# Strassen's scheme, one level, for the two feed-forward products of a transformer-like layer on one Trainium2 core

## The chip, the core and the metric

The kernel runs on one core of a Trainium2 chip. The core has five engines that run side by side, each through its own list of instructions from the first to the last: TensorE (PE) for matrix products and transposes, VectorE (DVE), ScalarE (ACT), GpSimd (POOL) and SyncE (SP). SP does no arithmetic here; it issues transfers between the chip's memory (DRAM) and SBUF, the core's working memory. TensorE writes to PSUM, eight banks of 128 x 512 float32. Engines wait for each other through semaphores. The metric is the device time of one execution in microseconds; lower is better.

## The reference, cut to what matters

One layer on 1024 tokens with 1024 channels: a normed projection, three mixers (a gated convolution, a stick-breaking attention, a cross-attention into 256 memory tokens), their gated sum, an output projection, and then the feed-forward part:

```python
        x = x + merged @ w_out[l]

        h2 = rms_norm(x, g_mlp[l])
        x = x + jnp.square(jax.nn.relu(h2 @ w_up[l])) @ w_down[l]
```

Here `h2` is 1024 x 1024, `w_up` 1024 x 4096 and `w_down` 4096 x 1024. The change touches only these two products and what surrounds them.

## The kernel before, in words

**Operands.** Every float32 operand is kept as two fp32r parts, a rounded part (hi) and what rounding left (lo). One product of a 128 x 128 block by a 128 x 512 block is three matmuls: hi by hi, hi by lo, lo by hi (`mm3` and `mm3_steps`, lines 125 to 127 and 205 to 207). To make the two parts, ACT copies with rounding (line 89 for a loaded weight of 128 x 1024, line 113 elsewhere) and DVE subtracts (lines 90 and 114). A product of weights therefore waits for ACT, and then for DVE behind ACT.

**Pools.** Weights are loaded by SP into `raw` (4 buffers of 128 x 1024), their two parts go to `whl` (3 buffers, each holding both parts of one load). Nearly everything else lives in `pg`, 40 pages of 128 x 1024 float32. PSUM is dealt out as `d` (3 banks), `z` (2), `t` (2) and `o` (1). Short-lived 128 x 512 tiles are in `hp` (3 buffers).

**Order.** The kernel's text is a recording: a scheduler turns it into one list for each engine, in the order of the text as far as buffers and its own estimate of times allow. The lists are fixed before the program runs, and an engine that waits at one row does none of the rows behind it.

**The output projection** (line 794) adds `merged @ w_out` to the rows of `x`, eight tiles of 128 rows (`acc`, one page each, kept in SBUF to the end). As each of them is done in its second half, `normed` (lines 157, 146, 150, 159) makes the normed row tile. `norm_transpose` (line 178 on PE, lines 116 and 117 for the two parts) turns the row tiles into `h2`, first those of the first 512 tokens, woven into the last tiles of the output projection, then those of the other 512, woven into the first matmuls of the feed-forward part.

**The feed-forward part** is a loop over 8 chunks of 512 inner columns. For each chunk: four blocks of 128 inner columns, each by two token halves, eight k-blocks and three matmuls (192 matmuls); ACT takes relu (line 812) and the square's hi part (line 815), DVE squares (816) and subtracts (817). Then, for two column halves and eight token tiles, four inner blocks by three matmuls (192 matmuls), and DVE adds the bank to `acc` (line 833). The inner result never leaves SBUF. In the last chunk each half tile of `acc` goes out as soon as its add is done (line 835). In all there are 3072 matmuls of 128x512.

Of the kernel before, what the change touches and what calls it, by code (L numbers as in the profile page):

```python
# [16 lines left out]
P = 128  # L17
# [5 lines left out]
NXH = 4  # L23
NM = M // P
FF = 4096
NCHUNK = FF // 512
EPS = 1e-6


# [7 lines left out]
def f32v(ap):  # L37

    return ap.bitcast(F32)
# [3 lines left out]
def block_kernel(ctx, tc, x, mem, small, w_in, w_v, w_kv, w_co, w_so, w_xo, w_out, w_up, w_dn, out):  # L43
# [19 lines left out]
    def page(dt=F32R, shape=(P, 1024)):  # L63
        return pgp.tile(list(shape), dt, tag="pg", name=nm("pg"))
# [41 lines left out]
    def unit(src, paged=False):  # L106

        return halves(load(src), paged)
# [63 lines left out]
    def norm_transpose(rows, dst, gcol):  # L172

        n = len(rows) * P
        for k in range(KT):
            tp = pt()
            for i, r in enumerate(rows):
                nc.tensor.transpose(tp[:, i * P : (i + 1) * P], r[:, k * P : (k + 1) * P], ident)
# [576 lines left out]

    acc = [None] * 8
    rows = []
    h2 = [None] * KT

    def h2_dst(th):  # L760
        def dst(k):
            if th == 0:
                h2[k] = {}
            t_ = page(F32R, (P, 2, 512))
            h2[k][th] = (t_[:, 0, :], t_[:, 1, :])
            return h2[k][th]

        return dst

    for ch in range(2):  # L770
        s = slice(ch * 512, ch * 512 + 512)
        while len(wo) < 4 * ch + 4:
            wo.append(unit(w_out[ch, len(wo) - 4 * ch], True))
        for t in range(8):
            th, i = t // 4, t % 4
            if ch == 0:
                acc[t] = page(F32)
                nc.sync.dma_start(out=acc[t], in_=x[t * P : (t + 1) * P, :])
            ps = pd()
            steps = mm3_steps(  # L780
                ps,
                [
                    (cut(mT[k, th], i * P, (i + 1) * P), cut(wo[4 * ch + k // 2], (k % 2) * 512, (k % 2) * 512 + 512))
                    for k in range(KT)
                ],
                4,
            )
            if ch == 1 and t == 5:
                more = norm_transpose(rows[0:4], h2_dst(0), C_GMLP)
# [10 lines left out]
    for c in range(NCHUNK):  # L800
        f = {}
        for j2 in range(2):
            ws = [unit(w_up[4 * c + 2 * j2 + j]) for j in range(2)]
            for th, j in ((0, 0), (0, 1), (1, 0), (1, 1)):
                w = ws[j]
                ps = pd()
                steps = mm3_steps(ps, [(cut(w, k * P, (k + 1) * P), h2[k][th]) for k in range(KT)], KT)
                if (c, j2, th, j) == (0, 0, 0, 1):
                    weave(steps, norm_transpose(rows[4:8], h2_dst(1), C_GMLP))
                run(steps)  # L810
                r = hpp.tile([P, 512], F32, tag="hp", name=nm("r"))
                nc.scalar.activation(r, ps, AF.Relu)
                t_ = page(F32R, (P, 2, 512))
                f[2 * j2 + j, th] = (t_[:, 0, :], t_[:, 1, :])
                nc.scalar.activation(t_[:, 0, :], r, AF.Square)
                nc.vector.tensor_tensor(out=r, in0=r, in1=r, op=ALU.mult)
                nc.vector.tensor_tensor(out=t_[:, 1, :], in0=r, in1=f32v(t_[:, 0, :]), op=ALU.subtract)
        for ch in range(2):
            us = [unit(w_dn[c, ch, kp]) for kp in range(2)]
            s = slice(ch * 512, ch * 512 + 512)  # L820
            for t in range(8):
                ps = pd()
                mm3(
                    ps,
                    [
                        (
                            cut(f[j, t // 4], (t % 4) * P, (t % 4 + 1) * P),
                            cut(us[j // 2], (j % 2) * 512, (j % 2) * 512 + 512),
                        )
                        for j in range(4)  # L830
                    ],
                )
                nc.vector.tensor_tensor(out=acc[t][:, s], in0=ps, in1=acc[t][:, s], op=ALU.add)  # L833
                if c == NCHUNK - 1:
                    nc.sync.dma_start(out=out[t * P : (t + 1) * P, s], in_=acc[t][:, s])


def _layout(i):
# [10 lines left out]
    def per_part(v):  # L849
# [9 lines left out]
    w_dn = a["w_down"][0].reshape(NCHUNK, 2, 2, P, 2, 512).transpose(0, 4, 1, 3, 2, 5)  # L859
    return {  # L860
        "x": a["x"][0],
        "mem": a["mem"][0],
# [9 lines left out]
        "w_dn": w_dn.reshape(NCHUNK, 2, 2, P, 1024),  # L872
    }


# [17 lines left out]
```

## Time and profile before

| what | value |
| --- | --- |
| time, median of 3 runs | 2309.98 us (2309.84 to 2311.8) |
| the profiled execution's own time | 2309.64 us |
| its span in the profile | 2307.9 us |
| PE busy | 2261.2 us (98% of the span) |
| DVE, ACT, POOL busy | 1130.1, 803.3, 303.3 us |
| bytes moved | 174.79 MB, mean 76 GB/s |
| last matmul of the output projection starts | 1603.44 us |
| last matmul of all starts | 2303.57 us |

In the profile a row of a group of instructions gives the line, the engine, the operation, what it writes and reads, the shape, the count, and then busy time in us, the mean of one in ns, and the engine's idle time just before such instructions with what ended it. The time of a matmul in these rows is from its start to its end; successive matmuls overlap, so their spacing has to be read from counts in a window. A row of the timeline gives the start and the duration in us.

### The profile page before, as it was taken

What the parts mean: (1) busy time and instruction counts of PE and PEld (TensorE: products, weight loads), DVE (VectorE), ACT (ScalarE), POOL (GpSimd) and SP (SyncE); (2) the same over time, 40 slices, a digit from 0 to 9 for tenths busy, and PEclk for the clock granted to TensorE, in tenths of its full rate; (3) what the DMA queues carried; (4) which work ended last, traced back from release to release, by engine and by line L of the source; (5) the groups of instructions that cost most, each with busy time, mean ns of one, the idle gap of its engine ahead of it and who ended that gap; (6) DMA issues with size and microseconds to landing.
All of it is one profiled execution on the core that took longest, in us unless ns stands there. A gap on an engine that the chain in (4) does not pass through costs nothing.

```text
span 2307.9 us, 26972 instructions
## 1 busy us (share of the span) xinstructions
PE 2261.2 (98%) x10688; PEld 1880.7 (81%) x10688; DVE 1130.1 (49%) x1589; ACT 803.3 (35%) x1550; POOL 303.3 (13%) x422
## 2 busy tenths in 40 slices
PE   7999999999999999999999999999999999999999
PEld 6988888778778778788888888888888888888887
DVE  5534127787777777763333344443333333333333
ACT  6544235565556555541122121223221221221221
POOL 1021113333334333320000000000000000000000
PEclk9999999999999999999999999999999999999999
DMA  6311322222122122211111443250111111111111
GB/s 220 101 60 68 125 69 76 72 75 81 64 83 73 65 90 65 83 40 52 46 47 63 146 156 128 92 191 1 37 55 55 37 55 52 40 55 48 44 46 73
DMA packets 49455, 174.79 MB, mean 76 GB/s; under 512 B 6065, under 2 KB 6065, under 8 KB 49329
## 3 DMA queue, kind: packets, MB, share of 16 engines
q1 hardware_dynamic: 42160, 147.90, 20.4%
q0 software_dynamic: 7168, 25.17, 2.9%
q8 instruction: 84, 1.38, 0.2%
q14 instruction: 43, 0.34, 0.0%
HBM read 135.29 MB, written 29.36 MB: 71 GB/s over the span
## 4 chain that ended last, share of the span: by engine, by line
PE 82%; DVE 6%; issue 5%; POOL 4%; ACT 3%; DMA 1%; SPq 0%; POOLq 0%; ACTq 0%; DVEq 0%
PE d L205 16%; PE d L207 16%; PE d L206 16%; PE d L125 9%; PE d L127 9%; PE d L126 9%; POOL pg L558 3%; PE o L597 2%; DVE pg L114 1%; PE t L582 1%; DVE pg L572 1%; ACT pg L555 1%; PE z L554 1%; PE z L553 1%; DVE pg L568 1%
## 5 line engine op out<-in xcount | busy, mean ns | idle before, releaser
L205 PE MATMUL d<-pg,whl 128*128 128x512 f32 x1664 | 655.2, 394 | 0.0
L207 PE MATMUL d<-pg,whl 128*128 128x512 f32 x1664 | 649.8, 391 | 0.0
L206 PE MATMUL d<-pg,whl 128*128 128x512 f32 x1664 | 649.4, 390 | 0.0
L207 PEld LDWEIGHTS d<-pg,whl 128*128 128x128 f32 x1664 | 312.4, 188 | 66.5
L206 PEld LDWEIGHTS d<-pg,whl 128*128 128x128 f32 x1664 | 312.7, 188 | 60.1
L205 PEld LDWEIGHTS d<-pg,whl 128*128 128x128 f32 x1664 | 312.7, 188 | 60.1
L90 DVE TENSOR_TENSOR whl<-raw,whl 128x1024 fp32r<-128x1024 f32 x160 | 201.9, 1262 | 302.3 <-ACT whl L89 301.8
L89 ACT CAST whl<-raw 128x1024 fp32r<-128x1024 f32 x160 | 168.6, 1054 | 518.4 <-PE d L127 291.5
L558 POOL TENSOR_SCALAR_AFFINE_SELECT pg<-pg 128x128 f32<-128x128 f32 x256 | 181.2, 713 | 317.4 <-ACT pg L555 301.6
L568 DVE TENSOR_TENSOR_SCAN pg<-pg,zero 128x128 f32<-128x128 f32 (+7 forms) x128 | 176.2, 1377 | 64.3 <-POOL pg L558 62.6
L127 PE MATMUL d<-whl,pg 128*128 128x512 f32 x512 | 199.2, 389 | 0.0
L125 PE MATMUL d<-whl,pg 128*128 128x512 f32 x512 | 199.2, 389 | 0.0
L126 PE MATMUL d<-whl,pg 128*128 128x512 f32 x512 | 199.2, 389 | 0.0
L113 ACT CAST pg<-t 128x256 fp32r<-128x256 f32 (+2 forms) x336 | 115.2, 364 | 212.4 <-DVE pg L114 144.7
L833 DVE TENSOR_TENSOR pg<-d,pg 128x512 f32<-128x512 f32 x128 | 88.3, 690 | 188.8 <-PE d L127 188.5
L114 DVE TENSOR_TENSOR pg<-t,pg 128x256 fp32r<-128x256 f32 (+2 forms) x336 | 129.4, 404 | 69.6 <-ACT pg L113 66.2
L126 PE MATMUL d<-pg,whl 128*128 128x512 f32 x384 | 149.4, 389 | 0.0
L125 PE MATMUL d<-pg,whl 128*128 128x512 f32 x384 | 149.4, 389 | 0.0
L127 PE MATMUL d<-pg,whl 128*128 128x512 f32 x384 | 149.4, 389 | 0.0
L205 PE MATMUL d<-pg,pg 128*128 128x512 f32 (+1 forms) x384 | 138.1, 360 | 1.3 <-ACT pg L116 1.3
L206 PE MATMUL d<-pg,pg 128*128 128x512 f32 (+1 forms) x384 | 136.9, 357 | 0.5 <-DVE pg L90 0.5
L207 PE MATMUL d<-pg,pg 128*128 128x512 f32 (+1 forms) x384 | 136.9, 357 | 0.0
(114 smaller groups left out, 2747.3 us busy)
## 6 DMA issues: line engine op xcount, KB each, us to landing
raw<-in_w_in SPq DMA_DIRECT2D x72, 512.0 KB, 3.6
raw<-in_w_up SPq DMA_DIRECT2D x32, 512.0 KB, 3.7
raw<-in_w_dn SPq DMA_DIRECT2D x32, 512.0 KB, 4.3
gscr<-pg POOLq DMA_DIRECT2D x24, 512.0 KB, 2.9
raw<-gscr SPq DMA_DIRECT2D x24, 512.0 KB, 3.3
raw<-in_w_kv SPq DMA_DIRECT2D x16, 512.0 KB, 4.4
pg<-in_x SPq DMA_DIRECT2D x16, 512.0 KB, 8.2
pg<-pg SPq DMA_DIRECT2D x32, 256.0 KB, 3.4
```

Of the source, the lines that this page charges most:

```text
L89: a = nc.scalar.copy(hl[0], raw)
L90: b = nc.vector.tensor_tensor(out=hl[1], in0=raw, in1=f32v(hl[0]), op=ALU.subtract)
L113: nc.scalar.copy(hi, src)
L114: nc.vector.tensor_tensor(out=lo, in0=src, in1=f32v(hi), op=ALU.subtract)
L125: nc.tensor.matmul(ps, lhsT=ah, rhs=bh, start=i == 0, stop=False)
L126: nc.tensor.matmul(ps, lhsT=ah, rhs=bl, start=False, stop=False)
L127: nc.tensor.matmul(ps, lhsT=al, rhs=bh, start=False, stop=i == n - 1)
L205: nc.tensor.matmul(ps, lhsT=ah, rhs=bh, start=i == 0, stop=False)
L206: nc.tensor.matmul(ps, lhsT=ah, rhs=bl, start=False, stop=False)
L207: nc.tensor.matmul(ps, lhsT=al, rhs=bh, start=False, stop=i == n - 1)
L558: nc.gpsimd.affine_select(out=t_[:, W - P : W], in_=t_[:, W - P : W], pattern=[[-1, P]], compare_op=ALU.is_gt, fill=fill_, base=0, channel ...
L568: nc.vector.tensor_tensor_scan(out=rev, data0=rev, data1=zero.broadcast_to([P, W]), initial=1.0, op0=ALU.mult, op1=ALU.add)
```

## The change

The two products are each done by seven products of half-size blocks instead of eight (Strassen's scheme in Winograd's form, one level), with sums and differences of blocks before and after.

**First product.** `h2` is cut into four blocks by channel half and token half, `w_up` by channel half and inner half. `h2_first` makes the blocks of the first 512 tokens (called "11" and "21"). `h2_second` makes the four mixed ones "t1" to "t4" and "22": DVE subtractions in float32 first (`vec`, line 771), then the parts (line 113 on ACT, 114 on DVE). `up_unit(u)`, 16 of them, loads the two halves of one strip of `w_up` (128 inner columns of either inner half), and does seven groups of 12 matmuls (`chain_mm`, lines 790 to 792) in two accumulating PSUM banks, a `d` bank and a `z` bank by turns. I number them P1 to P7: P1 and P2 use the weights as loaded, P3 and P4 the sums `sa`, P5 and P6 the differences `sb`, P7 the block `a22`. `sa` and `sb` are made by four DVE instructions; then ACT (line 89) and DVE (line 90) make their parts. Between the groups the banks are read, relu and square are taken by ACT in float32, and at the end four more DVE instructions form the sums that the second product needs.

**Inner result.** Seven blocks of 128 x 512 for each unit go to DRAM (`f_scr`, 112 stores of 256 KB, line 930) and are read back by the second product (56 loads of 512 KB, line 83 from `dn_first`). The rows of `x` after the output projection go to DRAM too (`x_scr`, line 858, issued by POOL) and are read back before the second product (line 956); their 8 pages are free during the first.

**Second product.** For each of four quarters of the inner dimension, seven products of 48 matmuls in four banks each (`banks_a`, `banks_c`, by turns). Each takes its left operand from `f_scr`, its right operand from blocks of `w_dn` (line 963) or from DVE sums of them; after each, DVE adds the four banks to `acc`, 28 adds of 128x512 in a quarter. The eight output tiles are stored whole at the end (line 1001). In all there are 2688 matmuls of 128x512. The transposes (64) are unchanged.

```diff
+    def vec(out, a, op, b):
+        nc.vector.tensor_tensor(out=out, in0=a, in1=b, op=op)
...
+    def h2_second(rows):
+        for kk in range(4):
+            r0, r1, ta, tb = h2_raw[kk], pair(), pair(), pair()
+            for j in range(2):
+                h2_tile(rows, kk + 4 * j, r1[:, j, :])
+                yield
+            vec(ta[:, 0, :], r1[:, 0, :], ALU.subtract, r0[:, 0, :])
+            vec(tb[:, 0, :], r1[:, 1, :], ALU.subtract, ta[:, 0, :])
+            vec(ta[:, 1, :], r1[:, 1, :], ALU.subtract, r1[:, 0, :])
+            vec(tb[:, 1, :], r0[:, 1, :], ALU.subtract, tb[:, 0, :])
+            h2["t2"][kk], h2["t4"][kk] = split_pair(tb)
+            h2["t1"][kk], h2["t3"][kk] = split_pair(ta)
...
+            split(r1[:, 1, :], *h2["22"][kk])
+            yield
...
             if ch == 1:
                 rows.append(normed(acc[t]))
+                nc.gpsimd.dma_start(out=x_scr[t], in_=acc[t])
...
+    def up_unit(u):
+        r1, r2 = load(w_up[u]), load(w_up[16 + u])
+        a11, a12, a21, a22 = r1[:, 0:512], r1[:, 512:1024], r2[:, 0:512], r2[:, 512:1024]
...
+        w = halves(r1)
+        xu, fa, fb, fc = pair(), pair(), pair(), pair()
+        a, c = pd(), pz()
+        chain_mm(a, op(w, 0), h2["11"], first=True)
+        nc.scalar.copy(xu[:, 0, :], a)
+        yield
+        chain_mm(c, op(w, 1), h2["21"], first=True, last=True)
+        vec(fa[:, 0, :], c, ALU.add, xu[:, 0, :])
...
+        act(fa[:, 0, :])
+        yield
+        sa, sb = pair(), pair()
+        vec(sa[:, 1, :], a21, ALU.add, a22)
+        vec(sa[:, 0, :], sa[:, 1, :], ALU.subtract, a11)
+        w = halves(flat(sa))
+        chain_mm(a, op(w, 0), h2["t2"])
+        nc.scalar.copy(xu[:, 1, :], a)
+        yield
+        c = pz()
+        chain_mm(c, op(w, 1), h2["t1"], first=True)
+        x5 = hpp.tile([P, 512], F32, tag="hp", name=nm("x5"))
+        nc.scalar.copy(x5, c)
+        yield
+        vec(sb[:, 0, :], a11, ALU.subtract, a21)
+        vec(sb[:, 1, :], a12, ALU.subtract, sa[:, 0, :])
+        w = halves(flat(sb))
+        chain_mm(a, op(w, 0), h2["t3"])
+        vec(fb[:, 1, :], a, ALU.add, x5)
+        act(fb[:, 1, :])
+        yield
+        chain_mm(c, op(w, 1), h2["22"], last=True)
+        vec(fa[:, 1, :], c, ALU.add, xu[:, 1, :])
+        act(fa[:, 1, :])
+        yield
...
+        chain_mm(a, op(w, 0), h2["t4"], last=True)
+        nc.scalar.activation(fb[:, 0, :], a, AF.Relu)
+        nc.scalar.activation(fb[:, 0, :], fb[:, 0, :], AF.Square)
...
+        vec(s4, fb[:, 0, :], ALU.subtract, fc[:, 1, :])
...
+            nc.sync.dma_start(out=f_scr[n, u // 4][:, u % 4, :], in_=t_)
...
+    for g in units[0:2]:
+        for _ in range(2):
+            next(g)
+            fill(second, 3)
+    run(second)
+    for g in units:
+        run(g)
...
+    for t in range(8):
+        acc[t] = page(F32)
+        nc.sync.dma_start(out=acc[t], in_=x_scr[t])
+    for q in range(NQ):
...
+        def product(banks, n, raws, to, first=False, last=False):
+            f, w = dn_first(n, q), dn_second(raws)
+            for i in range(4):
+                chain_mm(banks[i], [cut(hl, i * P, i * P + P) for hl in f], w, first, last)
+                t0, dh = to
+                t, s = t0 + i, slice(dh * 512, dh * 512 + 512)
+                vec(acc[t][:, s], banks[i], ALU.add, acc[t][:, s])
...
+        product(banks_a, "11", b11, (0, 0), first=True)
...
+        product(banks_a, "22", t_, (4, 0), last=True)
+        if q == NQ - 1:
             for t in range(8):
-                ps = pd()
...
+                nc.sync.dma_start(out=out[t * P : (t + 1) * P, :], in_=acc[t])
```

**Where the instructions now stand.** Three places matter later. A row gives line, operation, what is written and read, and the shape.

First place: DVE in the first product. Before, in a middle chunk, the list reads (`r` and `d` are the relu tile and its bank, `whl` the parts of the next weight):

```order
L816 TENSOR_TENSOR r_15879<-r_15879 128x512
L817 TENSOR_TENSOR pg_15881<-r_15879,pg_15881 128x512
L816 TENSOR_TENSOR r_15910<-r_15910 128x512
L817 TENSOR_TENSOR pg_15912<-r_15910,pg_15912 128x512
L90 TENSOR_TENSOR whl_15985<-raw_15983,whl_15985 128x1024
L816 TENSOR_TENSOR r_15941<-r_15941 128x512
```

Now, in unit 2: `z_13680` is the bank of P2, `pg_13676` holds f11 made from it, `raw_13668` and `raw_13670` are the two loads, `pg_13709` is `sa`, `pg_13710` is `sb`, `whl_13713` and `whl_13746` their parts, `whl_13812` the parts of unit 3's first load, `d_13679` the bank of P5:

```order
L771 TENSOR_TENSOR pg_13676<-z_13680,pg_13675 128x512
L771 TENSOR_TENSOR pg_13709<-raw_13670 128x512
L771 TENSOR_TENSOR pg_13710<-raw_13668,raw_13670 128x512
L771 TENSOR_TENSOR pg_13709<-pg_13709,raw_13668 128x512
L771 TENSOR_TENSOR pg_13710<-raw_13668,pg_13709 128x512
L90 TENSOR_TENSOR whl_13713<-pg_13709,whl_13713 128x1024
L90 TENSOR_TENSOR whl_13746<-pg_13710,whl_13746 128x1024
L90 TENSOR_TENSOR whl_13812<-raw_13808,whl_13812 128x1024
L771 TENSOR_TENSOR pg_13677<-d_13679,x_2172_13742 128x512
```

The four instructions that make `sa` and `sb` stand behind the one that reads P2's bank, although in what they read they need only the loads. Units 3 to 14 have the same nine rows with other numbers, unit 15 the first seven of them. On PE the last matmuls of P2 and the first of P3 follow each other:

```order
L791 MATMUL z_13680<-pg_13237,whl_13672 128x512
L792 MATMUL z_13680<-pg_13236,whl_13672 128x512
L790 MATMUL d_13679<-pg_13313,whl_13713 128x512
L791 MATMUL d_13679<-pg_13314,whl_13713 128x512
L792 MATMUL d_13679<-pg_13313,whl_13713 128x512
```

`whl_13713` is the left operand: the first two of P3's matmuls read its hi part, the third the lo part that DVE's L90 row writes. Nothing else stands on PE between the groups.

Second place: DVE at the start of the feed-forward part, the first quarter of `h2_second` and then the end of the last one with what follows (`pg_13294` and `pg_13102` are transposed rows of the second and first token half, `pg_13314` and `pg_13318` lo parts, `z_13280` is P2's bank of unit 0):

```order
L771 TENSOR_TENSOR pg_13295<-pg_13294,pg_13102 128x512
L771 TENSOR_TENSOR pg_13295<-pg_13294 128x512
L771 TENSOR_TENSOR pg_13296<-pg_13294,pg_13295 128x512
L771 TENSOR_TENSOR pg_13296<-pg_13102,pg_13296 128x512
L114 TENSOR_TENSOR pg_13314<-pg_13296,pg_13313 128x1024
L114 TENSOR_TENSOR pg_13318<-pg_13295,pg_13317 128x1024
L114 TENSOR_TENSOR pg_13322<-pg_13294,pg_13321 128x512
L771 TENSOR_TENSOR pg_13276<-z_13280,pg_13275 128x512
```

```order
L114 TENSOR_TENSOR pg_13461<-pg_13443,pg_13460 128x1024
L114 TENSOR_TENSOR pg_13465<-pg_13442,pg_13464 128x1024
L771 TENSOR_TENSOR pg_13470<-raw_13270 128x512
L771 TENSOR_TENSOR pg_13471<-raw_13268,raw_13270 128x512
L771 TENSOR_TENSOR pg_13470<-pg_13470,raw_13268 128x512
L771 TENSOR_TENSOR pg_13471<-raw_13268,pg_13470 128x512
L90 TENSOR_TENSOR whl_13474<-pg_13470,whl_13474 128x1024
```

All four quarters stand ahead of the parts of unit 0's `sa` (`whl_13474`). On PE, P1 and P2 of units 0 and 1 and the 32 transposes of the second token half stand ahead of unit 0's P3, and nothing more.

Third place: SP between the two products. Before, loads of `w_dn` follow loads of `w_up` with nothing between them:

```order
L83 DMA raw_15983<-in_w_up 128x1024
L83 DMA raw_16112<-in_w_dn 128x1024
L83 DMA raw_16117<-in_w_dn 128x1024
L83 DMA raw_16234<-in_w_dn 128x1024
```

Now the last store of unit 15 (`s_2396`, its last DVE result), seven of the eight loads of `x_scr` and then the first block of `w_dn`, which is the right operand of the second product's first matmuls, are in a row:

```order
L930 DMA fscr_s_3_12659<-s_2396_15616 128x512
L956 DMA pg_15630<-xscr_12625 128x1024
L956 DMA pg_15632<-xscr_12626 128x1024
L956 DMA pg_15634<-xscr_12627 128x1024
L956 DMA pg_15636<-xscr_12628 128x1024
L956 DMA pg_15638<-xscr_12629 128x1024
L956 DMA pg_15640<-xscr_12630 128x1024
L956 DMA pg_15642<-xscr_12631 128x1024
L963 DMA pg_15652<-in_w_dn 128x1024
L963 DMA pg_15654<-in_w_dn 128x1024
```

The loads of the first left operand from `f_scr` stand ahead of these rows.

More of the change, by code (lines that the diff above doesn't have):

```diff
@@ L757, in block_kernel @@
     rows = []
[L758 to L768, printed above, removed]
+    x_scr = [dram.tile([P, 1024], F32, name=f"xscr_{t}") for t in range(8)]
+    f_scr = {
+        (n, q): dram.tile([P, 4, 512], F32, name=f"fscr_{n}_{q}")
+        for n in ("11", "12", "22", "s1", "s2", "s3", "s4")
+        for q in range(NQ)
+    }
@@ L788, in block_kernel @@
             if ch == 1 and t == 5:
-                more = norm_transpose(rows[0:4], h2_dst(0), C_GMLP)
+                more = h2_first(rows[0:4])
             if ch == 1 and t >= 5:
@@ L796, in block_kernel @@
                 rows.append(normed(acc[t]))
+                nc.gpsimd.dma_start(out=x_scr[t], in_=acc[t])
     run(more)
[L800 to L805, printed above, removed]
-                ps = pd()
[L807 to L820, printed above, removed]
-            for t in range(8):
[L822 to L835, printed above, removed]
@@ new lines, in block_kernel, with dn_first @@
+    units = [up_unit(u) for u in range(16)]
+    second = h2_second(rows[4:8])
+    for g in units[0:2]:
[5 more added lines that the diff above has]
+        run(g)
+    def dn_first(n, q):
+        got = []
+        for kp in range(2):
+            hl = halves(load(f_scr[n, q][:, 2 * kp : 2 * kp + 2, :].rearrange("p a b -> p (a b)")))
+            got += [cut(hl, j * 512, j * 512 + 512) for j in range(2)]
+        return got
```

88 lines of the change are left out of this document (85 added, 3 removed).

## The prediction

> **What bounds the kernel now.** I read the head of the page and the chain of waits first, then the stretch of the feed-forward part by windows and by groups.
>
> ```profile
> span 2307.9 us, 26972 instructions
> PE 2261.2 (98%) x10688; PEld 1880.7 (81%) x10688; DVE 1130.1 (49%) x1589; ACT 803.3 (35%) x1550; POOL 303.3 (13%) x422
> PE 82%; DVE 6%; issue 5%; POOL 4%; ACT 3%; DMA 1%; SPq 0%; POOLq 0%; ACTq 0%; DVEq 0%
> ```
>
> TensorE is the bound. In a stretch inside the feed-forward part (columns: window, length, then busy time and count for PE, weight loads, DVE, ACT, POOL; granted clock, share of the transfer engines, GB/s):
>
> ```profile
> 1740.00:2200.00 460.00, 460.00 (x2032) 381.00 (x2031) 165.69 (x214) 89.37 (x123) 0.00 (x0) 1.00 0.16 49
> ```
>
> PE has no gap; one matmul takes 460.0 / 2032 = 0.2264 us. DVE is busy 36%, ACT 19%, transfers 16%. By groups, from 1560 us on:
>
> ```profile
> L207 PE MATMUL d<-pg,whl 128*128 128x512 f32 x512 | 199.2, 389 | 0.0
> L127 PE MATMUL d<-whl,pg 128*128 128x512 f32 x512 | 199.2, 389 | 0.0
> L833 DVE TENSOR_TENSOR pg<-d,pg 128x512 f32<-128x512 f32 x128 | 88.3, 690 | 188.8 <-PE d L127 188.5
> L90 DVE TENSOR_TENSOR whl<-raw,whl 128x1024 fp32r<-128x1024 f32 x61 | 74.6, 1223 | 141.1 <-ACT whl L89 141.1
> L89 ACT CAST whl<-raw 128x1024 fp32r<-128x1024 f32 x61 | 63.9, 1047 | 286.4 <-PE d L127 286.4
> L816 DVE TENSOR_TENSOR r<-r 128x512 f32<-128x512 f32 x64 | 44.0, 687 | 112.9 <-ACT pg L815 112.9
> L815 ACT ACTIVATE pg<-r 128x512 fp32r<-128x512 f32 x64 | 40.5, 632 | 1.0
> L812 ACT ACTIVATE r<-d 128x512 f32<-128x512 f32 x64 | 38.3, 598 | 244.8 <-PE d L207 244.8
> L116 ACT ACTIVATE pg<-t,sm 128x512 fp32r<-128x512 f32 x16 | 11.0, 687 | 9.7 <-PE t L178 9.6
> ```
>
> The matmuls never waited (0.0); DVE and ACT waited for PE. The question is whether that stays so when DVE gets more to do between a bank and the next operand.
>
> **What is removed.** 3072 matmuls become 2688: 384 x 0.2264 = **-86.9 us**, if PE stays fed.
>
> **The wait in every unit.** The third of P3's matmuls in a unit needs the lo part of `sa`. On DVE the four instructions that make `sa` and `sb` stand behind the add that reads P2's bank, and this add waits for P2's last matmul. So behind one wait for PE stand the operands for which PE itself comes next; during P2, when the loads are there and DVE has time, nothing of it is done. The hand-offs, from the timeline (start, duration):
>
> ```profile
> 2303.57 0.39 PE L127 MATMUL d<-whl,pg 128*128 128x512 f32 x1
> 2304.00 0.69 DVE L833 TENSOR_TENSOR pg<-d,pg 128x512 f32<-128x512 f32 x1 [2.03 <-PE d L127]
> 1624.49 1.04 ACT L89 CAST whl<-raw 128x1024 fp32r<-128x1024 f32 x1
> 1625.56 1.23 DVE L90 TENSOR_TENSOR whl<-raw,whl 128x1024 fp32r<-128x1024 f32 x1 [4.21 <-ACT whl L89]
> 1626.70 0.68 DVE L816 TENSOR_TENSOR r<-r 128x512 f32<-128x512 f32 x1
> 1627.42 0.69 DVE L817 TENSOR_TENSOR pg<-r,pg 128x512 fp32r<-128x512 f32 x1
> ```
>
> DVE starts 0.43 us after the start of a group's last matmul; from ACT to DVE it is 0.03 us; a DVE instruction that needs nothing of the one before starts 0.09 us before its end (1626.70 against 1626.79), one that does 0.04 us after it. From the start of P2's last matmul: add 0.43, `a21+a22` 1.03, `a11-a21` 1.63, `sa`'s second half 2.23 to 2.92; ACT's cast 2.95 to 4.00 (1.047 us; the relu and square of f11 on ACT are over by then, 0.43 + 0.69 + 2 x 0.63 = 2.4); DVE's lo part 4.03 to 5.26. The third matmul starts at 5.3 and without the wait would have started at 3 x 0.226 = 0.68: 4.6 us, with the weight load ahead of it **4.7 us**. The rest of a unit holds: P5's operand is ready at about 6.5 and P5 starts at 5.3 + 22 x 0.226 = 10.3; banks alternate, so each has a group's time (12 x 0.226 = 2.7 us) to be read in, and ACT (about 9.5 us by the rows) and DVE (about 12 us) are far below a unit's 84 x 0.226 + 4.7 = 23.7 us. Unit 1's P3 waits behind unit 0's last DVE result in the same way (relu, square, subtraction, three sums, cast, lo: about 5 us). So 15 units: 15 x 4.7 = **+70.5 us**. Bounds: 3.8 if the hi part alone decided, 5.3 if every hand-off took 0.1 us more: 57 to 80.
>
> **The start.** The last normed row tile is there, by the way it went before, 3.7 us after the next matmul could start:
>
> ```profile
> 1603.44 0.39 PE L207 MATMUL d<-pg,pg 128*128 128x512 f32 x1
> 1606.63 0.75 DVE L159 TENSOR_SCALAR pg<-pg,st 128x1024 f32<-128x1024 f32 x1 [0.66 <-POOL st L150]
> 1609.79 0.60 PE L178 MATMUL t<-ident,pg 128*128 128x128 f32 x4
> 1610.14 0.48 PE L205 MATMUL d<-pg,whl 128*128 128x512 f32 x1
> 1610.46 0.39 PE L206 MATMUL d<-pg,whl 128*128 128x512 f32 x1
> ```
>
> With the transposes and ACT's copy (0.687) DVE starts on the second half at 5.4. Each quarter is four subtractions of 0.69, a wait of 1.05 for the cast, two lo parts of 1.22 and one of 0.69: 6.9; four of them 27.8, two adds for P2 1.4, then three sums, cast and lo of unit 0's `sa` 4.3: 33.5, less 0.09 for some twenty unbound pairs, 31.7. P3 of unit 0 starts at 37.1. PE has until then 48 matmuls (10.9) and 8 groups of four transposes at 0.44 (from 1609.79 to 1610.46, less one spacing): 14.4. 37.1 - 14.4 = **+22.7 us**; bounds 18 (DVE's bare 29 us with casts hidden) to 26. Before, the same weaving cost PE nothing.
>
> **Between the products.** After unit 15's last group come relu, square and a subtraction, 0.2 + 0.6 + 0.63 + 0.69 = 2.2 us, and only then SP gets to seven loads of `x_scr` and to the first block of `w_dn`. Such a row of eight loads stands in the trace:
>
> ```profile
> L778 SPq DMA_DIRECT2D pg<-in_x x8: 377/411/588, 1514.6 to 1518.0; - x8
> DMA to landing us min/median/max: 4.5/7.3/10.0
> 1520.00:1530.00 10.00, 10.00 (x46) 8.29 (x45) 2.04 (x4) 0.57 (x1) 0.00 (x0) 1.00 1.01 406
> ```
>
> The eighth is issued 3.5 us after the first, the slowest lands after 10.0, and the engines are then full (share 1.01, 406 GB/s). The first block of `w_dn` stands eighth in its row: 2.2 + 3.5 + 10.0 = 15.7, the cast 1.05, the lo part 1.22, together 18.0, less the two hi matmuls that can go before the lo part (0.45): **+17.5 us**. Bounds: 12 if it lands as early as the quickest of the row (4.5), 21 if the stores of unit 15 and the other loads behind it (ten in all, not eight, at 406 GB/s: 2.6 us more) share the time. The two loads of `f_scr` for the first left operand stand ahead; what they read was written by the first four units.
>
> **Inside the second product.** In a quarter DVE has 28 adds of 0.69, 28 lo parts of 1.22 and 8 sums of 1.22: 63 us against 7 x 48 x 0.2264 = 76 us on PE, 83%. ACT's 28 casts take 29 us. PE waits only where a product's operand is made behind the last bank's add of the product before: by the order, the margin is there 0.1 to 0.5 us, and where two sums stand ahead of it 0.3 too little; the first products start with nothing made ahead, about 0.8 each. **+4 us**, bounds 0 and 32: the upper one is a whole exposed lo part, 1.22 less 0.03, at each of 27 boundaries.
>
> **The tail.** The last store is 512 KB in place of 256:
>
> ```profile
> out<-pg SPq DMA_DIRECT2D x16, 256.0 KB, 2.0
> raw<-in_w_up SPq DMA_DIRECT2D x32, 512.0 KB, 3.7
> raw<-in_w_dn SPq DMA_DIRECT2D x32, 512.0 KB, 4.3
> ```
>
> A load twice that size took 1.7 us more than the store, with other loads beside it; alone I take a third of that, **+0.6 us**; bounds 0 and 1.7.
>
> **What I cost at nothing.** A unit moves 2 loads of 512 KB and 7 stores of 256 KB, 2.9 MB in 23.7 us or 122 GB/s; a quarter about 11 MB in 76 us, 145 GB/s: both under half of the 406 GB/s above. SP's nine issues at 0.41 take 3.7 us of a unit's 23.7. Loads are issued a unit ahead and land in 3.7 us; if that cover went, a unit would wait those 3.7 us more (56 in all), but nothing before them on SP waits for the current unit's P3. The stores of `x_scr` are issued by POOL ahead of the norm's own POOL instruction (line 150); such an issue takes
>
> ```profile
> L621 POOL DMA_DIRECT2D gscr<-pg x24: 548/571/582, 347.0 to 975.2; - x24
> ```
>
> 0.57 us, and DVE needs longer than that for the instructions that line 150 waits for. ACT's copies of banks stand in the 9.5 us above.
>
> **The clock.** In all slices of the page the granted clock reads 9, which is 90% or more; only the matmuls at the start of the program run slower than the same ones later:
>
> ```profile
> PEclk9999999999999999999999999999999999999999
> 11.85 0.41 PE L205 MATMUL d<-pg,pg 128*128 128x256 f32 x1
> 12.06 0.41 PE L206 MATMUL d<-pg,pg 128*128 128x256 f32 x1
> 14.30 0.41 PE L205 MATMUL d<-pg,pg 128*128 128x256 f32 x1
> 19.07 0.28 PE L206 MATMUL d<-pg,pg 128*128 128x256 f32 x1
> 19.19 0.28 PE L207 MATMUL d<-pg,pg 128*128 128x256 f32 x1
> PE t L178 <- DVE pg L159: 10.4, 4, 7.8
> PE z L553 <- DVE pg L523: 7.4, 7, 1.2
> ```
>
> They are 0.21 us apart at first, 0.12 later; the slow ones (0.41) last until 14.30, 3.0 us from the first dense ones, and ahead of them lies the long wait of 7.8 at the program's start. I take it for a low clock after idleness. After the waits of 22 and 17 us I expect it again, at 1.3 us (3.0 x (1 - 0.12 / 0.21)) to 2.7 each: **+4 us**. The waits in the units I take as too short: they are broken by two hi matmuls, 3.6 us and then 0.8. After the start no wait of that length stands in this trace (the next in the list are 1.2 at most), so it shows neither case. The Trainium skill, "TensorE: Matmul & The Clock Gate", section "Why this matters for your kernels", speaks against the change: it wants no idle of TensorE over about 3 us between bursts, since one window of idle brings the clock down to half. By that rule each unit's 3.6 us could do it, and the sum would be that of the first rival below.
>
> **Sum.** -86.9 + 70.5 + 22.7 + 17.5 + 4 + 0.6 + 4 = +32.4; 2309.64 + 32.4 = **2342 us**. The profiled execution's 2309.64 is 1.7 over its span and 0.3 under the median 2309.98.
>
> **Rivals.**
>
> *The waits in the units also lower the clock.* For it: the slow matmuls at the start follow an idle stretch, and 15 waits leave TensorE idle 3.6 us in one piece. Against: the idle at the start was 7.8 us, twice that, and here PE is dense on both sides. Price: 1.3 us as at the start, up to all of P3 at half rate (12 x 0.226 = 2.7), times 15: +20 to +41, 2362 to 2383, middle 2372.
>
> *The second product is bound by DVE's hand-offs.* For it: 83% busy, where any add that waits for its bank pushes the next lo part. Against: banks alternate between products and the parts of the next operand are begun during the current one. Price: one lo part exposed at 27 boundaries, 32 us less the 4 counted: 2370.
>
> *Faster than before.* One mechanism: the operand `sa` costs less wait than I count, in each of 15 units. It decides at (86.9 - 22.7 - 17.5 - 4 - 0.6) / 15 = 2.8 us a unit: below it the change is faster. Without any wait there the time is 2342 - 70.5 = 2271 us. For it: no transfer is needed, and all of `sa`'s inputs are there early; PE's 84 matmuls of a unit take 19.0 us, DVE's work 12. Against: add, two of the four sums, cast and lo part follow each other strictly and each has its duration in a row above; the hi part alone needs 3.6.
>
> *It doesn't remove what it says.* 2688 matmuls of 128x512 stand in the changed program; this is excluded.
>
> **How the numbers follow.** The forecast 2342 has 0.55, with its own range 2320 to 2362 (units 57 to 80, transition 12 to 21, start 18 to 26, added as independent errors). Lowered clock in the units: 0.22. DVE's hand-offs: 0.10. Faster: 0.10. The rest, 0.03, lies where smaller gains cancel the waits, near no change; 0.2%, 4.6 us, is about what a measurement of this kernel tells from no change. The range 2318 to 2385 takes in the first two rivals and leaves out the faster case and the upper corner where two of them add.
>
> **What would show it right or wrong.** In the profile after, the waits should show PE before line 792 or 790 in the units held by the parts of `sa` (lines 89 and 90), 15 times some 4.5 us and no more than 5.3; one wait of about 22 us after the second unit's P2, with DVE fully busy in it; one of 17 before the first matmul of the second product, ended by line 90 behind a `w_dn` load. PE's busy time should fall by 87 us and the stretch from 1603.7 to the last matmul grow from 700 to about 732. Windows of single units at a granted clock under 0.95 would show the first rival; waits over 1 us at most product boundaries the second; waits in the units under 2.8 us the third, and then the forecast is wrong in its largest term.

## The result, and the profile after

The changed kernel takes 2374.3 us (median of 4, 2372.5 to 2374.9) where the kernel before takes 2310.4 in the same runs: a ratio of 1.0274, 95% interval 1.0257 to 1.0292. It is slower by 64 us. The forecast was slower by 32 us, at 2342; the range 2318 to 2385 holds the time, and it lies 2 us beside the first rival (2372), in which the waits in the units also lower the clock.

The head of the page after (span; busy time of the engines; granted clock in 40 slices, in tenths):

```profile
span 2372.4 us, 27104 instructions
PE 2224.2 (94%) x10304; PEld 1832.8 (77%) x10304; DVE 1313.7 (55%) x1781; ACT 954.4 (40%) x1726; POOL 308.1 (13%) x430
PEclk9999999999999999999999999998899899799999
```

384 matmuls are gone, yet TensorE is only 37 us less busy, not 87: some of the matmuls that are left got longer. The clock column says which: it reads 7 to 9 in the slices of the feed-forward part, where before it was 9 throughout. In the first product (units 1 to 15; columns as before, the clock follows POOL's busy time):

```profile
1654.00:2010.00 356.00, 299.24 (x1150) 234.78 (x1149) 156.99 (x209) 140.77 (x207) 0.00 (x0) 0.89 0.34 113
```

The mean clock is 0.89, where the row of before from 1740 to 2200 had 1.00. The waits of TensorE from 1595 us on (us in total, times, longest):

```profile
PE d L790 <- ACT whl L89: 71.8, 16, 15.0
PE d L790 <- ACT pg L113: 19.6, 1, 19.6
PE t L801 <- ACT pg L802: 4.0, 1, 4.0
PE d L792 <- DVE whl L90: 3.9, 8, 0.5
PE t L801 <- DVE pg L159: 1.4, 1, 1.4
PE z L792 <- DVE whl L90: 1.3, 2, 0.9
PE z L790 <- ACT whl L89: 0.6, 1, 0.6
```

The first row is the start (15.0) and 15 waits in the units (56.8, or 3.8 each). The second is the gap between the products. The row of line 792 with the bank `d` is the wait for the lo part of `sa`, in eight of the units. One unit, by TensorE, DVE and ACT (start, duration):

```profile
1679.67 0.39 PE L792 MATMUL z<-pg,whl 128*128 128x512 f32 x1
1683.79 0.79 PE L790 MATMUL d<-pg,whl 128*128 128x512 f32 x1 [3.73 <-ACT whl L89]
1685.05 0.79 PE L792 MATMUL d<-pg,whl 128*128 128x512 f32 x1
1686.07 0.63 PE L791 MATMUL d<-pg,whl 128*128 128x512 f32 x1
1686.49 0.63 PE L792 MATMUL d<-pg,whl 128*128 128x512 f32 x1
1690.49 0.39 PE L790 MATMUL z<-pg,whl 128*128 128x512 f32 x1
1690.72 0.39 PE L791 MATMUL z<-pg,whl 128*128 128x512 f32 x1
1680.16 0.69 DVE L771 TENSOR_TENSOR pg<-z,pg 128x512 f32<-128x512 f32 x1 [3.52 <-PE z L792]
1683.77 2.36 DVE L90 TENSOR_TENSOR whl<-pg,whl 128x1024 fp32r<-128x1024 f32 x2 [0.39 <-ACT whl L89]
1682.69 1.99 ACT L89 CAST whl<-pg 128x1024 fp32r<-128x1024 f32 x2 [0.51 <-DVE pg L771]
```

TensorE stands still for 3.73 us, and then the matmuls follow each other at 0.42 to 0.43 us (1686.07, 1686.49) in place of 0.23 (1690.49, 1690.72), until about 1690. So each wait is paid twice: once standing, once running slowly. Then the ends of the two products:

```profile
1602.76 0.39 PE L790 MATMUL d<-pg,whl 128*128 128x512 f32 x1
1639.04 0.80 PE L790 MATMUL d<-pg,whl 128*128 128x512 f32 x1 [14.97 <-ACT whl L89]
2036.32 0.39 PE L792 MATMUL d<-pg,pg 128*128 128x512 f32 x1
2056.28 1.22 PE L790 MATMUL d<-pg,whl 128*128 128x512 f32 x2 [19.57 <-ACT pg L113]
2367.43 0.39 PE L792 MATMUL o<-pg,whl 128*128 128x512 f32 x1
2056.00:2062.00 6.00, 5.68 (x13) 4.00 (x14) 5.67 (x5) 3.24 (x4) 0.00 (x0) 0.50 0.89 352
2080.00:2300.00 220.00, 218.12 (x956) 178.50 (x956) 180.87 (x195) 86.88 (x87) 0.00 (x0) 1.00 0.47 158
```

These are the first matmul of the first product, the first P3, the last matmul of the first product, the first and the last of the second, and two windows of the second. From them the account against the forecast:

| term | forecast | measured | how |
| --- | --- | --- | --- |
| matmuls removed | -86.9 | -86.9 | the undisturbed spacing is still 0.23 |
| start | +22.7 | +21.9 | 1639.04 - 1602.76 - 14.4 of work |
| waits in units 1 to 15 | +70.5 | +71 | as the forecast counted: P3's third matmul starts 5.38 after the start of P2's last one (5.85 in unit 1, 5.73 in unit 7) in place of 0.68 |
| between the products | +17.5 | +19.7 | 2056.28 - 2036.32 - 0.23 |
| inside the second product | +4 | +4 | 311.2 from first to last, less 304.1 of work, less the 3 of slow clock |
| tail | +0.6 | +0.6 | 2372.4 - 2367.43 against 2307.9 - 2303.57 |
| slow clock | +4 | +36 | a remainder: first product, 433.6 from first to last, less 307.6 of work and transposes, 21.9 and 71, leaves 33, of which about 31 in the units and 2 behind the start; behind the gap between the products (clock 0.50 in 6 us) 3 |
| waits of before that went, first product started earlier | 0 | -2 | before: 699.9 from first to last, less 698.8 of work; start at 1602.76 for 1603.67 |
| sum | +32 | +64 | the spans differ by 64.5 |

### The profile page after: what moved, and what is told of

It reads as the page before. It is cut to its first block, busy times and chain, and to the rows that moved or that the text cites. A ratio compares the mean times of both kernels' runs of the same rounds, so it can differ in the third digit from the quotient of the medians.

```text
span 2372.4 us, 27104 instructions
## 1 busy us (share of the span) xinstructions
PE 2224.2 (94%) x10304; PEld 1832.8 (77%) x10304; DVE 1313.7 (55%) x1781; ACT 954.4 (40%) x1726; POOL 308.1 (13%) x430
## 4 chain that ended last, share of the span: by engine, by line
PE 74%; DVE 10%; issue 6%; ACT 4%; POOL 4%; DMA 1%; SPq 0%; POOLq 0%; DVEq 0%; ACTq 0%
PE d L205 10%; PE d L207 10%; PE d L206 10%; PE d L792 5%; PE d L790 4%; PE d L791 4%; PE d L125 4%; PE d L127 4%; PE d L126 4%; POOL pg L558 3%; PE z L792 3%; PE z L790 3%; PE z L791 3%; DVE pg L771 2%; DVE pg L114 2%
## 5 line engine op out<-in xcount | busy, mean ns | idle before, releaser
L205 PE MATMUL d<-pg,whl 128*128 128x512 f32 x1152 | 455.3, 395 | 0.0
L206 PE MATMUL d<-pg,whl 128*128 128x512 f32 x1152 | 450.4, 391 | 0.0
L207 PE MATMUL d<-pg,whl 128*128 128x512 f32 x1152 | 450.3, 391 | 0.0
L89 ACT CAST whl<-raw 128x1024 fp32r<-128x1024 f32 x168 | 176.5, 1054 | 336.0 <-PE d L207 82.8
L90 DVE TENSOR_TENSOR whl<-raw,whl 128x1024 fp32r<-128x1024 f32 x168 | 210.2, 1258 | 179.0 <-ACT whl L89 178.4
L207 PEld LDWEIGHTS d<-pg,whl 128*128 128x128 f32 x1152 | 216.3, 188 | 46.4
L790 PE MATMUL d<-pg,whl 128*128 128x512 f32 x384 | 164.1, 428 | 91.3 <-ACT whl L89 71.8
L205 PEld LDWEIGHTS d<-pg,whl 128*128 128x128 f32 x1152 | 216.5, 188 | 40.6
L206 PEld LDWEIGHTS d<-pg,whl 128*128 128x128 f32 x1152 | 216.6, 188 | 40.3
L113 ACT CAST pg<-pg 128x1024 fp32r<-128x1024 f32 (+1 forms) x104 | 92.3, 900 | 199.6 <-DVE pg L749 53.3
L792 PE MATMUL d<-pg,whl 128*128 128x512 f32 x384 | 164.9, 431 | 4.2 <-DVE whl L90 3.9
L790 PEld LDWEIGHTS d<-pg,whl 128*128 128x128 f32 x384 | 79.4, 207 | 113.7 <-ACT whl L89 78.5
L791 PE MATMUL d<-pg,whl 128*128 128x512 f32 x384 | 161.8, 421 | 0.0
L125 PE MATMUL d<-pg,whl 128*128 128x512 f32 x384 | 149.4, 389 | 0.0
L126 PE MATMUL d<-pg,whl 128*128 128x512 f32 x384 | 149.4, 389 | 0.0
L127 PE MATMUL d<-pg,whl 128*128 128x512 f32 x384 | 149.4, 389 | 0.0
L205 PE MATMUL d<-pg,pg 128*128 128x512 f32 (+1 forms) x384 | 138.2, 360 | 0.4 <-ACT pg L116 0.4
L206 PE MATMUL d<-pg,pg 128*128 128x512 f32 (+1 forms) x384 | 137.0, 358 | 0.5 <-DVE pg L90 0.5
```

The costliest lines, as they stand in the source:

```text
L90: b = nc.vector.tensor_tensor(out=hl[1], in0=raw, in1=f32v(hl[0]), op=ALU.subtract)
L113: nc.scalar.copy(hi, src)
L125: nc.tensor.matmul(ps, lhsT=ah, rhs=bh, start=i == 0, stop=False)
L126: nc.tensor.matmul(ps, lhsT=ah, rhs=bl, start=False, stop=False)
L127: nc.tensor.matmul(ps, lhsT=al, rhs=bh, start=False, stop=i == n - 1)
L205: nc.tensor.matmul(ps, lhsT=ah, rhs=bh, start=i == 0, stop=False)
```

## The experiments

**What the clock costs in the units.** In units 1 to 15 matmuls that nobody needs fill the wait before P3:

```diff
         w = halves(flat(sa))
+        c = pz()
+        for _ in range(16 if u else 0):
+            nc.tensor.matmul(c, lhsT=h2["11"][0][0][:, 0:P], rhs=h2["21"][0][0], start=True, stop=True)
         chain_mm(a, op(w, 0), h2["t2"])
```

> The changed kernel, with 16 matmuls of 128x512 more in each of units 1 to 15, between P2 and P3. They read finished blocks of h2 and write a bank that P4 overwrites, so they wait for nothing and their result is not used. 16 x 0.2264 = 3.6 us of work stand where TensorE was idle for 3.7 us. Theory 1 (the idle stretch lowers the clock, and the slow matmuls behind it are what the forecast missed): the waits for the parts of sa end at the same moment as before, the granted clock stays at 1.00 through the units, and some 2.7 us a unit go: 2374 - 40 = about 2334. Theory 2 (the missing time lies in longer hand-offs on DVE and ACT, the clock is only a symptom): no change, 2370 to 2378. If the dummies delayed the unit themselves it would be slower than 2374.

2340.7 us, ratio 1.0133 (1.0118 to 1.0148): 33.6 us less than the changed kernel, by *adding* 240 matmuls. The window of the units, the wait that is left from 1650 to 1990 us, and then one unit from P2's last matmul to P3's third:

```profile
1654.00:1970.00 316.00, 312.86 (x1346) 250.01 (x1345) 154.95 (x208) 139.71 (x204) 0.00 (x0) 1.00 0.39 127
PE d L790 <- ACT whl L89: 1.0, 2, 0.6
1682.98 0.39 PE L792 MATMUL z<-pg,whl 128*128 128x512 f32 x1
1687.10 0.50 PE L790 MATMUL d<-pg,whl 128*128 128x512 f32 x1
1687.90 0.40 PE L791 MATMUL z<-pg,whl 128*128 128x512 f32 x1
1688.36 0.50 PE L792 MATMUL d<-pg,whl 128*128 128x512 f32 x1
```

The clock is 1.00 through the units, though the parts of `sa` come as late as before: P3's first and third matmuls start 4.12 and 5.38 us after P2's last one, as in the changed kernel. Theory 1 holds: time was lost to the clock. The gain is 2.2 us a unit, less than the 2.7 it named. Not quite all of it is the clock's. With `c` taken earlier, in this run and the next two, PE's list has P4's first two matmuls (the one at 1687.90 is the second) ahead of P3's third, so 2 x 0.23 = 0.45 us of work fills the wait for the lo part too. By the table above the clock cost about 31 / 15 = 2.1 us a unit.

**How long an idle stretch must be.** The same with fewer matmuls.

> As the run with 16 added matmuls, but with 6: 1.36 us of work, so TensorE's idle stretch in each of units 1 to 15 is about 2.4 us in place of 3.7. Theory 1a (only an idle stretch of about 3 us or more lowers the clock): clock 1.00 in the units, time as with 16, about 2334. Theory 1b (any wait of a few us lowers it): clock as in the changed kernel, about 0.86 to 0.93 in windows of 25 us, time near 2374. Theory 2 (the clock costs nothing): 2370 to 2378 for both.

> As the runs with 16 and 6 added matmuls in units 1 to 15, with 11: 2.5 us of work, so TensorE's idle stretch before P3 is about 1.2 us, where 16 left none, 6 left 2.4 and none added left 3.7. The kernel before had waits of up to 1.2 us without a change of the granted clock. Theory 1 (the clock falls with the length of the idle stretch, and 1.2 us is below what matters): clock 1.00 in the units and the time of 16 matmuls, 2338 to 2344. Theory 2 (any idle stretch at the same place lowers it in some units, in proportion to its length): clock about 0.98, between the two, 2344 to 2349.

With 6, 2348.5 us (1.0168, 1.0153 to 1.0183); with 11, 2341.3 us (1.0134, 1.0117 to 1.0151), the same as with 16. For 6 matmuls the window of the units, their waits, the first matmul of P3 in two neighbouring units, and a window of each of these units; then window and waits for 11:

```profile
1654.00:1980.00 326.00, 291.49 (x1219) 233.15 (x1218) 155.05 (x207) 139.57 (x204) 0.00 (x0) 0.97 0.38 122
PE d L790 <- ACT whl L89: 34.0, 14, 2.8
1684.05 0.80 PE L790 MATMUL d<-pg,whl 128*128 128x512 f32 x1 [2.37 <-ACT whl L89]
1708.65 0.50 PE L790 MATMUL d<-pg,whl 128*128 128x512 f32 x1 [2.37 <-ACT whl L89]
1684.00:1687.00 3.00, 2.95 (x7) 2.37 (x8) 2.97 (x3) 1.90 (x2) 0.00 (x0) 0.50 0.54 176
1707.00:1731.00 24.00, 20.97 (x90) 16.74 (x90) 11.84 (x17) 10.34 (x17) 0.00 (x0) 1.00 0.39 121
```

```profile
1654.00:1970.00 316.00, 296.91 (x1274) 236.75 (x1274) 154.99 (x207) 139.99 (x204) 0.00 (x0) 1.00 0.40 127
PE d L790 <- ACT whl L89: 19.4, 15, 1.7
```

Idle stretches of 1.3 us (19.4 / 15; the longest 1.7) leave the clock at 1.00. Stretches of 2.4 us give a mean of 0.97: after the same wait of 2.37 us one unit goes on at 0.50 (0.80 us for the first matmul) and the next at 1.00 (0.50 us, as in the run with 16). At 3.8 us the mean is 0.89. These means hide what happens. In the units of these traces the granted clock is either 1.00 or 0.50. With 6 matmuls it is 0.50 for 3.4 us in 7 of the 15 units and stays at 1.00 in the other 8; in the changed kernel it is 0.50 for 3.4 or 6.8 us in each of the 15. In both runs the starts of these slow stretches lie whole multiples of 3.41 us apart (1660.0, 1683.9 and 1731.7 us, the first three with 6 matmuls, are 7 and 14 times 3.41 apart). So where a wait falls on such a grid may decide whether it lowers the clock; no run here moves a wait to show it.

So neither theory of the run with 6 was right as put: 2.4 us is neither harmless nor as dear as 3.7, it costs about 8 us in all. In the run with 11 theory 1 holds (2338 to 2344); on theory 2 the time should have stayed above 2344.

**Taking the wait away.** The four instructions for `sa` and `sb`, and the parts of `sa`, are written at the start of the unit:

```diff
         w = halves(r1)
+        sa, sb = pair(), pair()
+        vec(sa[:, 1, :], a21, ALU.add, a22)
+        vec(sa[:, 0, :], sa[:, 1, :], ALU.subtract, a11)
+        vec(sb[:, 0, :], a11, ALU.subtract, a21)
+        vec(sb[:, 1, :], a12, ALU.subtract, sa[:, 0, :])
+        ws = halves(flat(sa))
         xu, fa, fb, fc = pair(), pair(), pair(), pair()
...
-        sa, sb = pair(), pair()
-        vec(sa[:, 1, :], a21, ALU.add, a22)
-        vec(sa[:, 0, :], sa[:, 1, :], ALU.subtract, a11)
-        w = halves(flat(sa))
+        w = ws
...
-        vec(sb[:, 0, :], a11, ALU.subtract, a21)
-        vec(sb[:, 1, :], a12, ALU.subtract, sa[:, 0, :])
```

> The changed kernel with one thing moved: the four DVE instructions that make sa and sb, and ACT's and DVE's parts of sa, are written at the start of the unit, ahead of P1 in the text and ahead of P2's add in DVE's list. Theory 1 (place in DVE's list makes the wait, and the wait makes the low clock): a unit falls from about 25.6 us to its 84 x 0.2264 = 19.0, 15 units give -98, so about 2276; the 15 waits ended by line 89 are gone and the clock is 1.00 in the units. Theory 2 (DVE or the weight buffers are the bound of a unit wherever the instructions stand): new waits at P3, P5 or P1 take at least half of it, 2325 or more. By the forecast's own terms without the clock: 2374 - 70 = 2304.

2264.2 us, ratio 0.9802 (0.9786 to 0.9819): the same arithmetic, 110 us faster than the changed kernel and 45 faster than the kernel before. The units now, and DVE in one of them around P2's last matmul (add at 1702.49, with the four instructions and the parts of `sa` ahead of it):

```profile
1654.00:1925.00 271.00, 271.00 (x1197) 223.55 (x1196) 157.70 (x215) 147.91 (x216) 0.00 (x0) 1.00 0.48 157
1700.60 0.68 DVE L771 TENSOR_TENSOR pg<-raw,pg 128x512 f32<-128x512 f32 x1
1701.34 1.23 DVE L90 TENSOR_TENSOR whl<-pg,whl 128x1024 fp32r<-128x1024 f32 x1
1702.49 0.69 DVE L771 TENSOR_TENSOR pg<-z,pg 128x512 f32<-128x512 f32 x1
```

TensorE is busy 271.00 of 271.00 us, at 271 / 1197 = 0.2264 us a matmul. The place of these instructions in the lists of DVE and ACT was the whole cause of the waits in the units: no new wait came at P3, P5 or P1, so theory 2 falls. Against the run with 16 filling matmuls, which has the waits without the clock, it is 76.5 us faster. About 9 us of this are the start's, since unit 0's `sa` also no longer stands behind the four quarters: here the first product takes 322.2 us from first to last, 14.6 more than its 307.6 of work, and in the changed kernel the start alone cost 23.8 (21.9 of waits and 1.9 of slow clock). The other 67 or so, with the 0.45 us a unit that P4's matmuls fill there, are near the forecast's 70.5 for the waits alone. The time is 12 us below what I expected of this run, most of it for the start.

**The gap between the products.** First the loads of the first block of `w_dn` ahead of the stored rows on SP:

```diff
+    early = block(0, 0, 0)
     for t in range(8):
         acc[t] = page(F32)
         nc.sync.dma_start(out=acc[t], in_=x_scr[t])
...
+        b11 = block(q, 0, 0) if q else early
```

> The changed kernel with the first two loads of w_dn ahead of the eight loads of the stored rows of x in SP's list; nothing else moves. Theory 1 (the queue of eight loads of 512 KB ahead of it is what the first product waits for): the wait of 19.6 us before the second product falls to 7 to 10 us, so about -10 to -12 and 2363. Theory 2 (the pages for these loads come free only with the last unit, and the loads' latency decides): the wait keeps 15 us or more, 2370 or above.

2373.1 us (1.0276, 1.0261 to 1.0291): no gain clear of the noise, though the wait fell, even below theory 1's 7 to 10 us. What TensorE and the others waited for from 2036 to 2110 us, and the window behind the gap:

```profile
2041.19 1.22 PE L790 MATMUL d<-pg,whl 128*128 128x512 f32 x2 [5.05 <-ACT pg L113]
2059.38 0.50 PE L790 MATMUL z<-pg,whl 128*128 128x512 f32 x1 [0.94 <-ACT pg L113]
2062.70 0.79 PE L791 MATMUL z<-pg,whl 128*128 128x512 f32 x1 [2.82 <-DVE pg L114]
2067.60 0.80 PE L790 MATMUL z<-pg,whl 128*128 128x512 f32 x1 [2.39 <-ACT whl L89]
2057.02 2.52 DVE L771 TENSOR_TENSOR pg<-pg,pg 128x1024 f32<-128x1024 f32 x2 [9.62 <-DMA pg<-in_w_dn]
2040.00:2065.00 25.00, 17.89 (x54) 12.43 (x54) 10.21 (x10) 4.18 (x4) 0.00 (x0) 0.80 0.83 316
```

The first product of the second part starts at 2041 instead of 2056. But the next block of `w_dn`, which the second one needs, is still behind the eight rows, and DVE waits 9.62 us for it; new waits of 2.8 and 2.4 us stand at the second product, and matmuls run slowly between them (clock 0.80 in 25 us). The gain was given back within the first two products.

Then all fourteen loads on POOL's queue, three blocks of `w_dn` before the rows, in the kernel with the operands formed early:

```diff
+    ready = [block(0, 0, 0, nc.gpsimd), block(0, 0, 1, nc.gpsimd), block(0, 1, 1, nc.gpsimd)]
     for t in range(8):
         acc[t] = page(F32)
-        nc.sync.dma_start(out=acc[t], in_=x_scr[t])
+        nc.gpsimd.dma_start(out=acc[t], in_=x_scr[t])
```

> The kernel with the operands formed early (2264 us), and the first six loads of w_dn, then the eight loads of the stored rows of x, issued by POOL in place of SP, in this order. POOL has nothing else to do there, so a load waits for its page only, not for the stores of unit 15 that stand ahead of it on SP. Theory 1 (the wait of 19.0 us before the second product is made by the place in SP's list): it falls to 5 us or less, the granted clock stays nearer 1.00, and the time is 2264 - 14 - 2 = about 2248. Theory 2 (pages come free too late): the wait keeps more than 10 us, and the time stays over 2256. Theory 3 (what was gained is given back at the second and third product, as in the run with the first two loads ahead): 2262 to 2266 with waits at the products behind.

2246.7 us, ratio 0.9725 (0.971 to 0.9739), as theory 1 said. SP's issue of the six loads of `w_dn` in the run before it (2264 us), then POOL's issues here, and what is left of the gap:

```profile
1933.37 6.62 SPq L964 DMA_DIRECT2D pg<-in_w_dn  x6
1904.94 0.58 POOL L959 DMA_DIRECT2D pg<-in_w_dn  x1 [298.38 <-DVE pg L771]
1914.98 1.05 POOL L959 DMA_DIRECT2D pg<-in_w_dn  x2 [4.13 <-DVE whl L90]
1925.10 0.53 POOL L966 DMA_DIRECT2D pg<-xscr  x1 [1.64 <-DVE whl L90]
1927.67 0.73 PE L790 MATMUL d<-pg,whl 128*128 128x512 f32 x2 [2.28 <-ACT pg L113]
```

The pages come free one by one during the last unit, and the loads go out then, where SP held them behind stores that wait for the unit's last sums. The gap falls from 19.0 to 2.3 us and nothing comes back later. This run changes two things at once, the queue and the order of blocks and rows; the three blocks ahead of the rows on SP were not tried, so what each is worth stays open. The same loads on POOL with the operands left late:

> The changed kernel (2374 us) with the fourteen loads before the second product issued by POOL, as in the run early_pool3, and the operands of the units left as late as they are. It tells whether the two costs add. Theory 1 (they are separate: the waits in the units, and the place of the loads in SP's list): the wait of 19.6 us before the second product falls to about 2.5, and the time by 17.5 as between early and early_pool3, to 2355 to 2359; the 15 waits in the units stay. Theory 2 (with TensorE waiting in each unit the loads were not late by themselves): under 8 us gained, over 2366.

2358.7 us (1.0208, 1.0193 to 1.0223), 15.6 less than the changed kernel, beside 17.5 less between the two runs with early operands. The two costs add, within the spread of this run's four times (2354.5 to 2362.1).

**The start.** Two tries in the kernels with early operands. Two subtractions of each quarter on POOL:

```diff
-            vec(ta[:, 1, :], r1[:, 1, :], ALU.subtract, r1[:, 0, :])
-            vec(tb[:, 1, :], r0[:, 1, :], ALU.subtract, tb[:, 0, :])
+            nc.gpsimd.tensor_tensor(out=ta[:, 1, :], in0=r1[:, 1, :], in1=r1[:, 0, :], op=ALU.subtract)
+            nc.gpsimd.tensor_tensor(out=tb[:, 1, :], in0=r0[:, 1, :], in1=tb[:, 0, :], op=ALU.subtract)
```

> The kernel with the operands formed early (2264 us), and two of the four subtractions of each quarter of h2_second done by POOL (128x512, about 1.3 us each by the row of line 251) in place of DVE (0.69 each). Theory 1 (DVE's own work sets the start of the first product; its waits there are about 8 us and its slow matmuls some 3): 8 x 0.69 = 5.5 us less on DVE, the time falls by 3 to 5, to about 2260. Theory 2 (the chain of one quarter sets it, and POOL's slower instruction lies in that chain): no gain or up to 5 slower, 2264 to 2270.

2265.9 us (0.9813, 0.9797 to 0.9829), not faster than 2264.2, as theory 2 said. Then three units ahead in place of two, in the kernel of 2246.7 us:

```diff
-    for g in units[0:2]:
+    for g in units[0:3]:
         for _ in range(2):
             next(g)
-            fill(second, 3)
+            fill(second, 2)
```

> The kernel of early_pool3 (2246.7 us) with P1 and P2 of three units instead of two ahead of the rest of h2_second, and two of a unit's pages taken only where they are first written. Some 6 us of waits and about 3.5 us of slow matmuls are left at its start of the first product. Theory 1 (TensorE there lacks independent work): 24 matmuls, 5.4 us, move into the waits, and the time falls by 4 to 9, to 2238 to 2243. Theory 2 (DVE sets the pace of the start, and a third unit's four instructions for sa and sb make it longer): no gain, 2244 to 2250.

2246.0 us (0.9723, 0.9707 to 0.9739), the same as without. The window of the start in this run:

```profile
1602.00:1627.00 25.00, 20.63 (x91) 14.99 (x91) 20.78 (x30) 14.82 (x21) 1.15 (x2) 0.93 0.21 73
```

DVE is busy 20.78 of 25 us. More work for TensorE ahead did not help, as theory 2 said, and less work for DVE did not help either where it was put on POOL; whether the order of the quarters (all of "t2" first) would, was not tried. The start's remaining cost stays open.

## Where the prediction was right, and the step that failed

**Removed: right.** Where TensorE is fed, a matmul costs 0.2264 us as before.

**The wait in every unit: right in place and size.** It was worked out from the order and the hand-offs of the trace as: cast from 2.95, hi part at 4.00, third matmul at 5.3 after the start of P2's last matmul. In the unit shown it is 1682.69 - 1679.67 = 3.02, 4.12 and 5.38. Fifteen waits came, ended by line 89. The term of 70.5 came out at 71. (The idle time on record is less, 56.8 + 3.9 us, because the two hi matmuls, which often ran slowly, filled most of the wait for the lo part.)

**Start, gap between the products, second product, tail: right within 2.3 us each.** The start's wait came in two pieces, 4.0 and 15.0 us around eight transposes, and not in one. The gap was a little longer (19.7 for 17.5), and its cause as forecast: seven rows and the first block in one row of loads on SP, behind unit 15's last sums. The second product is not bound by DVE; its boundaries wait 1.9 us in all.

**The clock: the step that failed.** I wrote of the waits in the units "I take as too short: they are broken by two hi matmuls, 3.6 us and then 0.8", and put 4 us for the clock at the two long waits alone. The clock came out at 36, about 31 of it in the units, and the run with 16 filling matmuls, which takes the idle stretch away, was 33.6 us faster. The hi matmuls break nothing: they come after the 3.7 idle us, and from the first of them, or at the latest by P3's third matmul, TensorE runs at half the clock. The one long wait in the trace of before was 7.8 us, so from it nothing could be said of 3.6; I took the unknown at its lower bound, though the rival's price, worked out from the same rows (1.3 to 2.7 a unit), was right: about 31 / 15 = 2.1. With that term at 2 x 15 = 30 the sum would have been 2372. The rule of the Trainium skill, "TensorE: Matmul & The Clock Gate", section "Why this matters for your kernels", which I had weighed and given 0.22, is what happened here: idle stretches of 3.7 us brought the clock down in the units. The runs add that stretches of 2.4 us did so in 7 of 15 units and stretches of 1.3 us in none.

So the sign was right for the reason given, the waits; the time was 32 us too low, because the slow matmuls behind the waits were put at almost nothing. That Strassen's scheme itself pays on this core is shown by the runs with early operands: the same 2688 matmuls, 2.0% and 2.75% faster than the kernel before.

## What to carry to other kernels

Count what an engine's list holds ahead of each operand, not what the operand needs: one add that waits for TensorE, standing ahead of work that waits for nothing, cost about 100 us in the units here (71 of waits, 31 of slow clock). An idle stretch of TensorE inside dense matmuls may have to be priced twice, once for itself and once for the slow matmuls behind it: here up to 1.7 us cost nothing more, 2.4 us did in about half of the units and 3.7 us in all. Where it can't be removed, even useless matmuls in it can gain. A load moved forward alone gained nothing here, because the next loads in need stayed behind; moving all of them, to a queue in which no late result stood ahead, gained 15.6 and 17.5 us.

## What the runs showed that was not expected

That the granted clock reacts to stretches as short as 2.4 us, there in 7 of 15 units, and then falls to half for 3.4 us (mean clock 1.00, 1.00, 0.97 and 0.89 in the units with idle stretches of 0, 1.3, 2.4 and 3.8 us). And that a kernel became 1.4% faster (2374.3 to 2340.7 us) by 240 matmuls whose result is thrown away.
